# A hybrid block on one core: weight stream first in the engine orders, magnitude sums on ScalarE in place of maxima on VectorE, group operand sums on VectorE, other pacing

## The chip, the core and the metric

The kernel runs on one core of a Trainium2 chip. The core has five engines that each work through their own list of instructions in order: TensorE (PE in the profile, matrix products, with a second row PEld for its weight loads), VectorE (DVE), ScalarE (ACT), GpSimd (POOL) and SyncE (SP, which here only issues transfers). An instruction that has to wait for another engine, a buffer or a transfer holds up everything behind it in its list. The metric is the device time of one execution in microseconds (us). The kernel before took 3001.04, 3008.76 and 3016.93 us in three runs, so its median is 3008.76 us. The profiled execution took 2998.34 us.

## What is computed

One layer of a sequence model over 2048 latent and 256 context tokens of 1024 channels. The reference, cut to its core:

```python
h = modulate(x, norm1_g, shift1, scale1)                  # RMSNorm, scaled and shifted by c @ w_ada
u, g, p, gt = split(h @ w_in)                             # 1024, 1024, 512 and 2048 columns
uc = depthwise_conv(u)                                    # 4 taps
for d in (forward, backward):                             # gated linear recurrence
    r, i = sigmoid(uc @ w_r[d] + b_r), sigmoid(uc @ w_i[d] + b_i)   # 16 blocks of 64x64
    a = exp(-8 * r * softplus(-lam)); b = sqrt(1 - a*a) * (i * uc)
    h_lru += scan(a, b, start=final state of the context tokens)
pm = pool_mixer(p)                                        # windows 2, 4, 8, 16 in rows of 64
z = h_lru * gelu(g)
y = (sigmoid(gt[:1024]) * (z @ w_lru_out) + sigmoid(gt[1024:]) * (pm @ w_pool_out)) @ w_o
x = x + gate1 * y
x = x + gate2 * (square(relu(modulate(x, norm2_g, shift2, scale2) @ w1)) @ w2)
return rms_norm(x, final_g)
```

Inputs, outputs and weights are float32.

## The kernel before

**Numbers in two halves.** Each operand of a large product is scaled by a power of two and written as a float16 high part and a float16 rest. A product is three float16 matmuls (high by high, high by rest, rest by high; `mm3`, L78 to L85). The power of two comes from a bound on the magnitude: per partition a maximum (`absmax`, L104, on VectorE), a matmul with ones that adds the 128 partitions (L93, tile `sm`, a single bank of PSUM), and three small VectorE instructions on its result (L97, L99, L101). ScalarE then writes the high part (L108) and VectorE the rest (L109). For an input weight the maximum is `wm` (L124, L522), for the convolved channels `um` (L618), for a finished product of recurrence and gate `zmax` (L682).

**First part, the branches** (matmuls of L83, up to 1182 us of the trace). The modulated input stays on chip. An iteration over 8 groups of 128 channels (L740 to L755) does for group j: the gates of the recurrence (matmuls on `slot` by `g`, sigmoids L638), with the u columns of the next group between them; the coefficients and scans (L654 to L667, ScalarE, VectorE and GpSimd); the loads of the next input weights (`fetch`); the convolution of the next group, its `um` and its split (L610 to L622); one fill (sigmoid gate columns, evacuated from PSUM by ScalarE, L567, and stored); and the gate columns with GeLU (L678), times the recurrence (L680, L681) and out to memory. PSUM has 7 banks for these products. The pool branch follows.

**Second part, the merge** (1182 to about 1760 us). From here on products are in Winograd's form: 2x2 blocks with 7 products in place of 8 (`Job`, L938). Its operands need sums of blocks. Three groups of tokens (684, 684 and 680) go through the projections po, lo and wo. `from_dram` (L877) loads the four blocks of an operand into a tile F, forms three sums in four subtractions (`t_sums`, L853) on GpSimd, and splits the seven blocks (L863, L864).

**Third part, the MLP** (from about 1760 us): three groups through w1 and w2, matmuls of L957 again.

**The weight stream.** The weights of po, lo, wo, w1 and w2 are 44 units. Each is prepared once: loaded raw (tile `praw`, `load_raw`, L239), bounded by two sums of magnitudes on ScalarE (L264), scaled, summed into its seven blocks on GpSimd (four instructions a quarter of 128 columns, L290 to L293, tiles `praw` and `psum`), split into halves by ScalarE (L296, L297) and VectorE (L300, two a quarter, tile `pout`), and stored to memory (L303, `st_...`). A quarter here is 128 of a unit's columns: four to a unit, two for the po units. Products load prepared units with L931 into `wu`, by `ensure`, always some units ahead of their use. `prepare` (L251) is a generator: each `yield` names a number of TensorE columns, and `pace` (L314), called after each product with its columns, runs the generator on when they are used up. So the stream is written into the program between the products. `ensure` runs it further where a unit is needed at once. In the first part there is one `praw` buffer, later there are two (`prep_pool`).

**What sets the order.** SyncE's list is the program's order (L61). For the other engines a scheduler orders instructions by when it expects them to be ready and by a priority, which follows the program's order; `tc.high_priority` puts instructions ahead. The sum matmul of the weight stream stays at its place in the program on TensorE (L95).

## Time and profile before

| | us |
|---|---|
| three runs | 3001.04, 3008.76, 3016.93 |
| profiled execution | 2998.34 |
| its span, first to last instruction | 2996.6 |
| TensorE busy | 2600.5 (87%) |
| VectorE busy | 2079.3 (69%) |
| ScalarE busy | 1401.2 (47%) |
| GpSimd busy | 989.2 (33%) |
| mean granted TensorE clock | 0.940 of full speed |

The chain of waits that ended last is TensorE's own for the most part, so what matters is where TensorE stands still. TensorE's idle time differs much between the three parts, and the rows below are therefore taken part by part. In a row of a group, the time after the bar is the engine's idle time just before these instructions, and what ended it.

### The profile page before, as it was taken

What the parts mean: (1) busy time and instruction counts of PE and PEld (TensorE: products, weight loads), DVE (VectorE), ACT (ScalarE), POOL (GpSimd) and SP (SyncE); (2) the same over time, 40 slices, a digit from 0 to 9 for tenths busy, and PEclk for the clock granted to TensorE, in tenths of its full rate; (3) what the DMA queues carried; (4) which work ended last, traced back from release to release, by engine and by line L of the source; (5) the groups of instructions that cost most, each with busy time, mean ns of one, the idle gap of its engine ahead of it and who ended that gap; (6) DMA issues with size and microseconds to landing.
All of it is one profiled execution on the core that took longest, in us unless ns stands there. A gap on an engine that the chain in (4) does not pass through costs nothing. (4 is left out here: it accounts for less than half of the span.)

```text
span 2996.6 us, 39247 instructions
## 1 busy us (share of the span) xinstructions
PE 2600.5 (87%) x15212; PEld 1513.3 (50%) x15212; DVE 2079.3 (69%) x3151; ACT 1401.2 (47%) x1912; POOL 989.2 (33%) x1103
## 2 busy tenths in 40 slices
PE   6798798787788798977677699999899999999997
PEld 2243344343343344644444466666566665566664
DVE  6759779876976865575846868786774657665656
ACT  4645664465558334455535655563432333432322
POOL 4513443452525413766847543331010000100001
PEclk9899999898899899989888899999899999999998
DMA  7022233132112325877578597775454343454442
GB/s 301 1 94 97 95 137 124 60 139 95 77 68 104 107 95 190 306 273 277 210 279 290 205 335 287 267 273 185 150 213 153 143 170 137 154 223 148 150 162 84
DMA packets 152572, 513.75 MB, mean 171 GB/s; under 512 B 14144, under 2 KB 55872, under 8 KB 148160
## 3 DMA queue, kind: packets, MB, share of 16 engines
q1 hardware_dynamic: 114640, 386.96, 36.1%
q10 hardware_dynamic: 37744, 124.27, 10.6%
q8 instruction: 119, 1.95, 0.3%
q14 instruction: 69, 0.57, 0.1%
HBM read 386.92 MB, written 124.26 MB: 171 GB/s over the span
## 5 line engine op out<-in xcount | busy, mean ns | idle before, releaser
L957 PE MATMUL mm<-C,wu 128*128 128x342 f16 (+1 forms) x10584 | 1602.1, 313 | 159.7 <-DVE xm L1021 33.2
L957 PEld LDWEIGHTS <-wu 128*128 128x128 f16 x10584 | 1041.6, 99 | 707.9 <-issue 131.4
L83 PE MATMUL mm<-A,w 128*128 128x512 f16 x3408 | 791.0, 392 | 65.3 <-ACT slot L567 22.4
L83 PEld LDWEIGHTS <-w 128*128 128x128 f16 x3600 | 362.7, 102 | 491.6 <-issue 101.2
L1021 DVE SCALAR_TENSOR_TENSOR xm<-mm,cs,xm 128x342 f32<-128x342 f32 (+1 forms) x672 | 371.9, 570 | 212.8 <-PE mm L957 204.1
L206 POOL TENSOR_TENSOR psum<-praw 128x128 f32<-128x128 f32 x336 | 226.7, 680 | 504.6 <-DVE pout L300 297.2
L1144 POOL TENSOR_TENSOR xm<-xm,E 128x342 f32<-128x342 f32 (+1 forms) x84 | 80.6, 985 | 921.7 <-ACT E L1143 921.7
L1004 ACT ACTIVATE E<-mm,ivj 128x342 f32<-128x342 f32 (+1 forms) x216 | 112.8, 540 | 289.3 <-PE mm L957 270.7
L296 ACT ACTIVATE pout<-praw,su 128x512 f16<-128x512 f32 x168 | 120.1, 717 | 254.1 <-POOL praw L291 111.6
L300 DVE SCALAR_TENSOR_TENSOR pout<-praw,su,pout 128x512 f16<-128x512 f32 x168 | 145.6, 869 | 97.8 <-ACT pout L296 94.2
L291 POOL TENSOR_TENSOR praw<-praw 128x128 f32<-128x128 f32 x168 | 127.9, 769 | 124.0 <-issue 65.9
L863 ACT ACTIVATE C<-F,sc_s 128x1368 f16<-128x1368 f32 (+1 forms) x96 | 116.2, 1281 | 102.9 <-DVE sc_s L101 100.2
L1012 DVE SCALAR_TENSOR_TENSOR F<-mm,ivj,E 128x342 f32<-128x342 f32 (+1 forms) x144 | 81.2, 568 | 117.0 <-PE mm L957 106.0
L300 DVE SCALAR_TENSOR_TENSOR pout<-psum,su,pout 128x384 f16<-128x384 f32 x168 | 143.6, 856 | 5.3 <-ACT pout L297 3.9
L206 DVE TENSOR_TENSOR F<-F 128x342 f32<-128x342 f32 (+1 forms) x240 | 127.0, 534 | 24.8 <-ACT F L1203 20.1
L864 DVE SCALAR_TENSOR_TENSOR C<-F,sc_s,C 128x1368 f16<-128x1368 f32 (+1 forms) x96 | 140.6, 1471 | 0.0
L83 PE MATMUL mm<-slot,g 128*128 128x512 f16 (+1 forms) x528 | 118.5, 370 | 15.3 <-ACT slot L638 11.7
L264 ACT ACTIVATE pout<-praw 128x1024 f16<-128x1024 f32 (+1 forms) x88 | 89.4, 1016 | 77.3 <-DMA st_w<-pout 26.1
L297 ACT ACTIVATE pout<-psum,su 128x384 f16<-128x384 f32 x168 | 101.3, 606 | 28.2 <-POOL psum L206 28.0
L638 ACT ACTIVATE slot<-mm,vec,ivg 128x512 f32<-128x512 f32 (+1 forms) x160 | 106.9, 736 | 11.8 <-PE mm L83 8.9
L1007 ACT ACTIVATE F<-mm,ivj 128x342 f32<-128x342 f32 (+1 forms) x48 | 26.0, 542 | 173.4 <-PE mm L957 173.4
L206 POOL TENSOR_TENSOR psum<-praw,psum 128x128 f32<-128x128 f32 x168 | 97.7, 589 | 6.3
(188 smaller groups left out, 2762.5 us busy)
## 6 DMA issues: line engine op xcount, KB each, us to landing
wu<-st_w SPq DMA_DIRECT2D x192, 896.0 KB, 6.3
st_w<-pout ACTq DMA_DIRECT2D x128, 448.0 KB, 4.9
praw<-in_w_dram SPq DMA_DIRECT2D x96, 256.0 KB, 5.5
slot<-in_w_ada_dram SPq DMA_DIRECT2D x22, 1024.0 KB, 8.7
wu<-st_lo SPq DMA_DIRECT2D x24, 896.0 KB, 10.5
wu<-st_wo SPq DMA_DIRECT2D x24, 896.0 KB, 11.0
s<-slot ACTq DMA_DIRECT2D x11, 1024.0 KB, 3.9
xm<-s SPq DMA_DIRECT2D x32, 342.0 KB, 9.6
```

The lines of the kernel that those rows point to most:

```text
L83: TE.matmul(ps, l, r, start=(c == 0), stop=(c == n - 1))
L206: e.tensor_tensor(o, x, y, op=OP.subtract)
L291: G.tensor_tensor(r[:, 3, c], r[:, 3, c], r[:, 2, c], op=OP.add)
L296: S.activation(u[q][:, 0, 0:4, :], r[:, :, c], AF.Copy, scale=su)
L297: S.activation(u[q][:, 0, 4:7, :], f[q], AF.Copy, scale=su)
L300: V.scalar_tensor_tensor(u[q][:, 1, lo:hi, :], x, su, u[q][:, 0, lo:hi, :], op0=OP.mult, op1=OP.subtract)
L638: S.activation(dst[:, o:o + w], ps[:, :w], AF.Sigmoid, bias=vcol("br" if i == 0 else "bi", 8 * d + j), scale=self.ivg)
L863: S.activation(c[:, 0, lo:hi, :w], f[:, lo:hi, :], AF.Copy, scale=s)
L864: V.scalar_tensor_tensor(c[:, 1, lo:hi, :w], f[:, lo:hi, :], s, c[:, 0, lo:hi, :w], op0=OP.mult, op1=OP.subtract)
L957: TE.matmul(ps, l, r, start=(first and k == 0 and i == 0), stop=(k == self.m - 1 and i == 2), skip_group_check=(bank != "Y"))
L1004: S.activation(e[n], ps, AF.Copy, scale=iv)
L1021: V.scalar_tensor_tensor(o, ps, cs(r), o, op0=OP.mult, op1=OP.add)
```

## The change

Five edits. (1) Every step of the weight stream is now issued at high priority (`advance`), where before only its scale was. (2) The maxima over input weights (`prep`, `small_weights`), convolved channels (`conv`) and finished products (`gate`) become sums of magnitudes by ScalarE's Abs with an accumulated output; the elementwise output goes into a tile that is written later anyway, or is no longer needed. (3) `from_dram`'s block sums go from GpSimd to VectorE. (4) A speed factor multiplies the columns in `pace`: 1.25 in the first part, 0.6 in the second, 1.15 in the third. (5) Two yields differ: 5000 in place of 5500 a step, and 12000 in place of 5000 after a unit where there is one `praw` buffer. The maxima in `pool_sums`, `pool_mix` and a few small ones stay.

```diff
--- before.py
+++ after.py
@@ -116,12 +116,14 @@
     def prep(srcs, joint=False, w16=None):
 
         k = len(srcs)
-        raws, m = [], sm.tile([P, k], F32, name=f"wm{k}")
+        raws, ts, m = [], [], sm.tile([P, k], F32, name=f"wm{k}")
         for i, src in enumerate(srcs):
             n = src.shape[-1]
             raw = ring.tile([P, 1024], F32, name="raw")
             nc.sync.dma_start(raw[:, :n], src)
-            absmax(m[:, i:i + 1], raw[:, :n])
+            t = ring.tile([P, 2, 1024], F16, name="w16") if w16 is None else w16[i]
+            S.activation(t[:, 0, :n], raw[:, :n], AF.Abs, accum_out=m[:, i:i + 1])
+            ts.append(t)
             raws.append(raw[:, :n])
         if joint:
             mj = sm.tile([P, 1], F32, name="wmj")
@@ -131,7 +133,7 @@
         out = []
         for i, raw in enumerate(raws):
             n = raw.shape[-1]
-            t = ring.tile([P, 2, 1024], F16, name="w16") if w16 is None else w16[i]
+            t = ts[i]
             split(t[:, 0, :n], t[:, 1, :n], raw, s[:, 0:1] if joint else s[:, i:i + 1])
             out.append(t)
         return out, inv
@@ -235,6 +237,7 @@
             prep_order += [("w2", 2 * q - 2), ("w2", 2 * q - 1)]
     prep_pool = [prep1, 1, 1, 2]
     rest = [0.0]
+    speed = [1.25]
 
     def load_raw(kind, i):
         pp, nraw, _, _ = prep_pool
@@ -267,8 +270,7 @@
             mj = sm.tile([P, 1], F32, name="wmj")
             V.tensor_tensor(mj, m[:, 0:1], m[:, 1:2], op=OP.add)
             yield 3000
-            with tc.high_priority(offset=PRIO):
-                s, inv = scale_of_(mj, 1, 14, True)
+            s, inv = scale_of_(mj, 1, 14, True)
             su = sm.tile([P, 1], F32, name="su")
             V.tensor_copy(su, s)
             V.tensor_copy(inv_u[:, BASE[kind] + i:BASE[kind] + i + 1], inv)
@@ -301,21 +303,22 @@
                                                    op0=OP.mult, op1=OP.subtract)
                     else:
                         nc.scalar.dma_start(t[:, q], u[q])
-                yield 5500
+                yield 5000
             stash[(kind, i)] = t
             if nraw == 1:
-                yield 5000
+                yield 12000
 
     prep_steps = prepare()
 
     def advance():
-        rest[0] += next(prep_steps, 1e12)
+        with tc.high_priority(offset=PRIO):
+            rest[0] += next(prep_steps, 1e12)
 
     def pace(columns):
 
         if rest[0] is None:
             return
-        rest[0] -= columns
+        rest[0] -= columns * speed[0]
         while rest[0] <= 0:
             advance()
 
@@ -519,7 +522,7 @@
         nc.sync.dma_start(raw, src)
         w16 = hcp.tile([P, 2, 512], F16, name="g16", bufs=2)
         m = sm.tile([P, 1], F32, name="wm1")
-        absmax(m, raw)
+        S.activation(w16[:, 0], raw, AF.Abs, accum_out=m)
         s, inv = scale_of(m, 1)
         split(w16[:, 0], w16[:, 1], raw, s)
         return w16, inv
@@ -615,9 +618,9 @@
             for k in range(1, 4):
                 V.scalar_tensor_tensor(uc, up[:, k:k + L], vcol("cw", 8 * k + j), uc, op0=OP.mult, op1=OP.add)
             um = sm.tile([P, 1], F32, name="um")
-            absmax(um, uc)
+            self.u16 = slot([P, 2, L], F16)
+            S.activation(self.u16[:, 0], uc, AF.Abs, accum_out=um)
             su, invu = scale_of(um, 1)
-            self.u16 = slot([P, 2, L], F16)
             split(self.u16[:, 0], self.u16[:, 1], uc, su)
             self.ivg = mul_small(invg, invu, 1, "ivg")
 
@@ -679,7 +682,7 @@
             z = self.h[1]
             G.tensor_tensor(z[:, 0:T], self.h[0][:, 0:T], z[:, 0:T], op=OP.add)
             V.tensor_tensor(z[:, 0:T], z[:, 0:T], gel, op=OP.mult)
-            absmax(zmax[:, j:j + 1], z[:, 0:T])
+            S.activation(gel, z[:, 0:T], AF.Abs, accum_out=zmax[:, j:j + 1])
             nc.scalar.dma_start(z_d[j], z[:, 0:T])
 
 
@@ -880,7 +883,7 @@
         f = f_tile(w)
         for src, sl in ((srcs[k], slice(0, 4, 3)), (srcs[k + half], slice(1, 3))):
             nc.sync.dma_start(f[:, sl, :], src[:, t0:t0 + 2 * w].rearrange("p (c t) -> p c t", c=2))
-        t_sums(G, f[:, 0, :], f[:, 1, :], f[:, 2, :], f[:, 3, :], f)
+        t_sums(V, f[:, 0, :], f[:, 1, :], f[:, 2, :], f[:, 3, :], f)
         return split_f(f, s, w)
 
     aff2 = affine(mod2[:, 2, :], mod2[:, 1, :], vc("g2"), 2, UP)
@@ -1263,6 +1266,7 @@
         for _ in range(n):
             next(it, None)
 
+    speed[0] = 0.6
     stages = [Stage(g) for g in range(3)]
     stages[0].y, stages[0].z = y_0, z_0
     for i in range(4):
@@ -1291,6 +1295,7 @@
             sg.wo(i)
             if nx:
                 nx.load_z(i)
+    speed[0] = 1.15
     for g in range(3):
         for p in range(8):
             if g or p:
```

In the first part the change moves ScalarE's instructions in each iteration. Here is ScalarE's list for the third convolution of the first part, before: `w_...` are split input weights, `g_...` the weights of the recurrence's gates, the L108 row with `slot` is the split of the convolved channels, L567 evacuates the fill and L678 the gate.

```order
L108 ACTIVATE w_2297<-raw,sc_s_2295 128x1024
L303 DMA st_po_2223<-pout 128x1792
L264 ACTIVATE pout,wm_2548<-praw 128x1024 x2
L108 ACTIVATE w_2312<-raw,sc_s_2310 128x1024
L108 ACTIVATE g_2317<-raw,sc_s_2326 128x512
L108 ACTIVATE slot<-slot,sc_s_2343 128x2312
L567 ACT_TABLE_LOAD
L567 ACTIVATE slot<-mm,ivf 128x512 x4
L678 ACT_TABLE_LOAD
L678 ACTIVATE slot<-mm,ivp 128x512 x2
```

And the same place in the list now, where L125, L525 and L622 are the new sums, and L570 is the old L567:

```order
L125 ACTIVATE w_2309,wm_2306<-raw 128x1024
L622 ACTIVATE slot,um<-slot 128x2312
L570 ACT_TABLE_LOAD
L570 ACTIVATE slot<-mm,ivf 128x512 x4
L125 ACTIVATE w_2324,wm_2321<-raw 128x1024
L525 ACTIVATE g_2338,wm_2339<-raw 128x512
L108 ACTIVATE w_2309<-raw,sc_s_2317 128x1024
L125 ACTIVATE w_2532,wm_2529<-raw 128x1024
L573 DMA s_5_150<-slot 128x2048
L108 ACTIVATE w_2324<-raw,sc_s_2332 128x1024
L108 ACTIVATE g_2338<-raw,sc_s_2347 128x512
L108 ACTIVATE slot<-slot,sc_s_2365 128x2312
```

The four evacuations of the fill have moved from behind the split of the convolved channels to behind their sum; the split of the gate weights (`w_2297` before, `w_2309` now) has moved from ahead of all this to behind the evacuations.

TensorE's list at the same place now, from the last matmul of the fill to the first ones of the gate (before, the four `sm` matmuls stood one by one between matmuls of the fill and the gate):

```order
L83 LDWEIGHTS w_1821
L83 MATMUL mm<-A_364,w_1821 128x512
L93 MATMUL sm<-wm_2306,ones 128x1
L93 MATMUL sm<-wm_2321,ones 128x1
L93 MATMUL sm<-wm_2339,ones 128x1
L93 MATMUL sm<-um,ones 128x1
L83 LDWEIGHTS w_2309
L83 MATMUL mm<-A_189,w_2309 128x512
```

The four sums stand together, and the gate's matmuls behind them need the split of `w_2309`. Such a row of four stands at three of the eight convolutions (the third, the fourth and the last); before, only the sixth has one. At the second, fifth, sixth and seventh the gate's weights are now split ahead of the sum over the channels.

In the second part SyncE's list changes in the number of raw loads. Before, in the third group of tokens, from the last loads of po on (`praw` is a raw unit, `wu` a prepared one, `xm` gate values):

```order
L248 DMA praw<-in_w_dram 128x2x256 x4
L931 DMA wu<-st_po_1912 128x3584
L1045 DMA xm<-s_0_153 128x2x340
L1045 DMA xm<-s_4_157 128x2x340
L931 DMA wu<-st_po_2223 128x3584
L1045 DMA xm<-s_1_154 128x2x340
L1045 DMA xm<-s_5_158 128x2x340
L248 DMA praw<-in_w_dram 128x2x256 x4
L931 DMA wu<-st_wo_4479 128x3584 x2
L1045 DMA xm<-s_2_155 128x2x340
L1045 DMA xm<-s_6_159 128x2x340
L931 DMA wu<-st_wo_4873 128x3584 x2
```

The same place now:

```order
L934 DMA wu<-st_po_1815 128x3584
L1048 DMA xm<-s_0_153 128x2x340
L1048 DMA xm<-s_4_157 128x2x340
L934 DMA wu<-st_po_2087 128x3584
L1048 DMA xm<-s_1_154 128x2x340
L1048 DMA xm<-s_5_158 128x2x340
L934 DMA wu<-st_wo_3940 128x3584 x2
L1048 DMA xm<-s_2_155 128x2x340
L1048 DMA xm<-s_6_159 128x2x340
L251 DMA praw<-in_w_dram 128x1024
L249 DMA praw<-in_w_dram 128x512 x2
L934 DMA wu<-st_wo_4283 128x3584 x2
```

Of the two raw loads within these rows one is left, further back. Counted by the matmuls on `wmj` in TensorE's list, 16 units are scaled ahead of the first product of the second part before and 20 now; in the second part 16 before and 10 now; in the third 12 before and 14 now.

## Rows read from the trace of the kernel before

**Rows 1.** Busy time, granted clock and DMA by part: PE, PEld, DVE, ACT, POOL, clock.

```profile
130.00:1182.00 1052.00, 902.00 (x4204) 425.39 (x4201) 784.80 (x797) 572.79 (x682) 395.19 (x312) 0.93 0.27 101
1182.00:1760.00 578.00, 442.59 (x2749) 278.74 (x2749) 375.41 (x613) 287.30 (x479) 376.19 (x495) 0.89 0.74 271
1760.00:2997.00 1237.00, 1171.09 (x7973) 777.22 (x7970) 820.48 (x1606) 475.76 (x652) 145.46 (x237) 0.98 0.51 185
```

**Rows 2.** What TensorE waited for, 1182 to 1760: total us, times, longest.

```profile
PE mm L957 <- ACT E L1004: 32.3, 12, 8.3
PE mm L957 <- DMA wu<-st_lo: 17.5, 4, 6.7
PE sm L93 <- DVE wmj L268: 17.0, 8, 5.6
...
PE mm L957 <- DMA wu<-st_po: 12.5, 3, 10.2
```

**Rows 3.** What SyncE's queue waited for, 1182 to 1760.

```profile
SPq L248 <- DVE pout L300: 224.3, 13, 34.3
```

**Rows 4.** SyncE's issues in order of time: start, us, line, transfer.

```profile
1548.45 1.07 SPq L931 DMA_DIRECT2D wu<-st_lo  x2
1573.86 0.33 SPq L248 DMA_DIRECT2D praw<-in_w_dram  x1
...
1575.44 1.63 SPq L882 DMA_DIRECT2D F<-z  x2
1577.17 1.31 SPq L931 DMA_DIRECT2D wu<-st_lo  x2
```

**Rows 5.** What TensorE waited for, 130 to 1182.

```profile
PE sm L93 <- DVE um L105: 34.4, 5, 10.6
...
PE mm L83 <- ACT slot L567: 22.4, 6, 12.3
```

**Rows 6.** Busy time around the third and the sixth convolution, columns as Rows 1.

```profile
331.00:398.00 67.00, 51.20 (x232) 23.53 (x231) 59.82 (x54) 30.17 (x34) 28.31 (x15) 0.90 0.32 116
...
640.00:718.00 78.00, 48.20 (x230) 23.77 (x228) 66.41 (x60) 33.20 (x38) 37.00 (x27) 0.80 0.20 75
```

**Rows 7.** VectorE's groups, 1182 to 1760: busy us, mean ns, idle before.

```profile
L300 DVE SCALAR_TENSOR_TENSOR pout<-praw,su,pout 128x512 f16<-128x512 f32 x63 | 54.8, 877 | 22.9 <-ACT pout L296 22.0 <-DMA praw<-in_w_dram 0.8
L300 DVE SCALAR_TENSOR_TENSOR pout<-psum,su,pout 128x384 f16<-128x384 f32 x63 | 51.7, 824 | 0.5 <-ACT pout L297 0.5
...
L206 DVE TENSOR_TENSOR F<-F 128x342 f32<-128x342 f32 x24 | 15.7, 655 | 3.8 <-ACT F L1170 3.5
```

**Rows 8.** GpSimd's groups, 1182 to 1760.

```profile
L206 POOL TENSOR_TENSOR F<-F 128x342 f32<-128x342 f32 (+1 forms) x56 | 54.0, 965 | 26.6 <-DMA F<-z 21.6 <-DMA F<-y 3.6
...
L291 POOL TENSOR_TENSOR praw<-praw 128x128 f32<-128x128 f32 x64 | 33.0, 527 | 32.5 <-issue 17.8 <-ACT pout L264 14.1
```

**Rows 9.** VectorE's groups, 130 to 1182.

```profile
L300 DVE SCALAR_TENSOR_TENSOR pout<-psum,su,pout 128x384 f16<-128x384 f32 x56 | 60.2, 1075 | 4.8 <-ACT pout L297 3.4
L300 DVE SCALAR_TENSOR_TENSOR pout<-praw,su,pout 128x512 f16<-128x512 f32 x56 | 53.8, 962 | 51.5 <-ACT pout L296 48.8 <-DMA s<-slot 2.6
...
L105 DVE TENSOR_REDUCE wm<-raw 128x1 f32<-128x1024 f32 (+1 forms) x37 | 40.0, 1099 | 36.5 <-DMA raw<-in_w_gl_dram 21.8 <-DMA raw<-in_pool_w_dram 7.1 <-DMA raw<-in_w_gt_dram 3.9
...
L105 DVE TENSOR_REDUCE um<-slot 128x1 f32<-128x2312 f32 (+1 forms) x12 | 29.5, 2460 | 0.1
...
L105 DVE TENSOR_REDUCE zmax<-slot 128x1 f32<-128x2048 f32 x8 | 18.2, 2281 | 0.1
```

**Rows 10.** ScalarE's groups, 130 to 1182.

```profile
L108 ACT ACTIVATE w<-raw,sc_s 128x1024 f16<-128x1024 f32 x32 | 36.6, 1147 | 22.2 <-DVE sc_s L101 22.2
...
L108 ACT ACTIVATE slot<-slot,sc_s 128x2312 f16<-128x2312 f32 (+1 forms) x12 | 25.8, 2148 | 113.8 <-DVE sc_s L101 113.8
L567 ACT ACTIVATE slot<-mm,ivf 128x512 f32<-128x512 f32 x41 | 25.5, 686 | 17.6 <-PE mm L83 17.5
```

**Rows 11.** GpSimd's groups, 130 to 1182.

```profile
L291 POOL TENSOR_TENSOR praw<-praw 128x128 f32<-128x128 f32 x55 | 67.6, 1229 | 46.5 <-ACT pout L264 38.7 <-issue 4.7
```

## The prediction

> **What bounds the kernel now.** I read the busy times by part first. TensorE is idle for 1052 - 902 = 150 us in the first part, 578 - 443 = 135 us in the second and 1237 - 1171 = 66 us in the third [rows 1]. The second part is the worst: 23% idle in a fifth of the time, and the granted clock is lowest there (0.89 of full speed, so some of it at 1.2 GHz in place of 2.4). The third part is 95% busy and has little to give. So each edit is judged by TensorE's idle time in the first two parts.
>
> In the second part no engine is full: VectorE 65%, GpSimd 65%, ScalarE 50%, DMA 74% [rows 1]. I then asked what TensorE waited for. The rows name late weights (17.5 and 12.5 us on prepared units of lo and po), the weight stream's own sum matmul `wmj`, 17.0 us, and evacuations by ScalarE, 32.3 us [rows 2]. Late weights have a cause one step back. SyncE, whose list is in program order, stood at the raw loads of the weight stream for 224.3 us in 13 waits, 17 us each, until VectorE had finished with an earlier raw unit (L300) and its buffer was free [rows 3]. The issues in order of time show one such wait: after the load of 1548.45 nothing leaves until 1573.86, when the raw load goes; the next prepared weights of lo, which do not depend on it at all, leave at 1577.17 [rows 4]. A low-priority VectorE instruction holds the buffer, the raw load holds SyncE, and TensorE's weights stand behind it.
>
> In the first part TensorE waited for the channel maximum `um`, 34.4 us, and for banks that ScalarE had not evacuated from the fill, 22.4 us [rows 5]. A stretch from one gate section to the next shows why: from 331 to 398 us VectorE is busy 59.8 of 67 us and TensorE only 51.2, and from 640 to 718 it is 66.4 of 78 and 48.2 [rows 6]. VectorE is the bound in these stretches.
>
> **The change, part by part: second part.** Pacing sets how many units are prepared here. A unit cost 8000 + 3000 + 4000 + 7 x 5500 = 53,500 columns, or 156 matmuls of 342; now it costs 50,000 / 0.6 = 83,300, or 244. The part's products have some 2500 matmuls, so 16 units become 10, as the order counts. The 63 quarters of before [rows 7] become 40. That takes 23 x (0.877 + 0.824) = 39 us off VectorE. The block sums of `from_dram` come onto it: 56 instructions [rows 8], at 0.655 us as VectorE does the same shape elsewhere [rows 7], 37 us. So VectorE stays as it is, and GpSimd loses the 54 us that these took there [rows 8] and its share of the stream.
>
> What I expect of the waits: raw loads stand 88 matmuls further apart, and a raw unit is released sooner, since its last VectorE instructions now come first. Both shorten SyncE's 17 us. Late weights and `wmj` together are 17.5 + 12.5 + 17.0 = 47 us [rows 2]; I take off four fifths, 38 us (bounds 0 and 47, none being the case that the transfers themselves are slow). Of the 32.3 us of evacuations I take 8, a quarter: the stream is cut by 23/63, but at high priority what is left now stands ahead of evacuations (bounds: 32 off, 32 on). The clock: a matmul here took 442.59/2749 = 161 ns against 1171.09/7973 = 147 ns in the third part [rows 1], 39 us in all. With a third of the idle time (46 of 135 us) gone, a third of it comes back, 13 us. Against this, F's transfers were waited for by GpSimd, 26.6 us [rows 8], where little stood behind. Now VectorE waits for them, with evacuations queued behind it that TensorE needs. I charge 10 (bounds 0 and 27). Second part: -38 - 8 - 13 + 10 = -49 us.
>
> **First part.** Maxima that leave VectorE: 40.0 us of `wm`, 8 of 12 `um` at 2.460 = 19.7, and 18.2 of `zmax` [rows 9], 78 us. Sums that come to ScalarE are not in the trace in this place; nearest are its passes over like shapes, 1.147 us for 1024 elements, 2.148 for 2312 and 0.686 for 512 [rows 10], so 28 x 1.147 + 9 x 0.686 + 16 x 2.148, about 73 us. The weight stream's pace is a quarter faster (a unit's 30,000 + 15,000 + 13 x 5500 + 5000 = 121,500 columns become 30,000 + 15,000 + 13 x 5000 + 12,000 = 122,000, over 1.25 97,600). 20 units stand ahead of the second part instead of 16, which is 16 more quarters. On VectorE they cost 16 x (1.075 + 0.962) = 33 us [rows 9]. VectorE is relieved by 45 us and ScalarE goes, with its part of the stream (some 30 us), from 573 [rows 1] to some 680 of 1052 us, still below two thirds.
>
> Where it counts is in the bound stretches. By the order, from the second L657 of an iteration to the split of the next channels, 7 `um` and 8 `wm` go (26 us) and 17 instructions of the stream come (17 us): -9. Next, the fill is evacuated behind the channels' sum and no longer behind their split, so I take 17 of the 22.4 us [rows 5]. Against this, ScalarE's sum waits for VectorE's convolution, and at three convolutions the gate's weights are split only behind it: TensorE reaches the end of the fill and has nothing to do. Before, only the sixth convolution has its four sums in a row like that. That stretch left TensorE idle for 78 - 48 = 30 us, the third convolution's for 67 - 51 = 16 [rows 6]: such a stop costs up to 14 us. Three in place of one are 28 us at most (0 at least, where the matmuls held back are done while something else is waited for later); I take half, 14. First part: -9 - 17 + 14 = -12 us (bounds -57, all of rows 5 gone, and +28, with one exception under the rivals).
>
> **Third part.** 14 units in place of 12, 7 quarters, 12 us of VectorE at the prices of rows 7, beside a TensorE that is 95% busy. Cover is VectorE's idle third (820 of 1237 us busy [rows 1]); I charge 2 us (0 to 12). The first 130 us, with eight of the input maxima, I leave as they are.
>
> Sum: -49 - 12 + 2 = -59 on the profiled execution's 2998.3 us, 2939 us. The median of before lies 10 us above that execution, and single runs spread from 3001 to 3017. I add half of the 10 and forecast 2945 us, with its own range of 2885 to 2995.
>
> **A rival on the slow side: ScalarE's list stops TensorE at every convolution.** ScalarE already stood 113.8 us before its 12 splits of channels [rows 10]. The new sum stands ahead of the split, waits for the same convolution, and has evacuations and weight splits behind it at all eight. If TensorE stops at all of them at 14 us each, that is 112 - 14 = 98 us, and the 9 and 17 us above do not come: 2998 + 98 - 49 + 2 = 3049 us. It decides the sign from four further stops on, since 4 x 14 exceeds the other parts' gain. Against it: at the second, fifth, sixth and seventh convolution the gate's weights are split ahead, so TensorE has some 20 us of gate matmuls to do meanwhile. 15%.
>
> **A rival with a smaller gain: VectorE and GpSimd hold each other up.** The same GpSimd instruction (L291) takes 1229 ns in the first part [rows 11] and 527 in the second [rows 8], and VectorE's L300 1075 against 824 [rows 9, 7]. The first part gets 16 x 4 more GpSimd instructions, 34 us at 527 ns and 79 at 1229; if the mean of 56 falls on VectorE for the share of time that it is bound (seven stretches of some 65 us in 1052, 43%), 24 us come on top: first part +12, 2998 + 12 - 49 + 2 = 2963 us, 2970 with the offset. 20%. The Trainium skill's page "SBUF — State Buffer", under "Who interferes with whom", says that on trn2 a `tensor_reduce` never contends with GpSimd, while a VectorE instruction with two inputs in SBUF does, with the later one blocked throughout. By that rule the change removes VectorE time that disturbed nobody and adds time that does, which speaks for this rival; the rows show the two prices but not which VectorE instruction caused them.
>
> **A rival near no change: the second part keeps its waits.** DMA is 74% busy there at 271 GB/s [rows 1]; if loads are late by their number and not by SyncE's wait, and the evacuations stay as they are, only the 8 us come: 2998 - 12 - 8 + 2 = 2980, 2986 with the offset. Against it: the quiet of 25 us in rows 4. 12%.
>
> **How the numbers follow.** The forecast has 53%, the three rivals 15, 20 and 12. 0.5% (15 us) is about what a measurement of this kernel can tell from no change, so faster means below 2994, slower above 3024. The forecast's case lies below 2994 nearly always, the second rival in five of six, the third in half: 0.75. The slow rival with its nearer end gives most of slower: 0.13. Same: 0.12. For 8 in 10 I take 2875 to 3020: at the lower end all of the 47 us, all of rows 5 and half more of the 32 go (2945 - 9 - 45 - 16 = 2875), the upper one covers the two small rivals and the near end of the slow one.
>
> **What would show it.** Right: SyncE's waits at raw loads in the second part fall to a third or less of 224 us; TensorE's idle time there falls from 135 to some 90 us and the clock rises above 0.91; L300 counts some 40 quarters there. In the first part, waits of TensorE for L567 nearly vanish and those for `um`'s successor name ScalarE. Wrong: SyncE's waits are gone and TensorE is idle as before (then the evacuations were the cause); VectorE's sums on F wait long for transfers with L1021 behind them; TensorE's idle time in the first part exceeds 180 us (the slow rival); or GpSimd's L291 rises above 1229 ns there (the second).

## The result and the profile after

The changed kernel takes 2986.14 us (median of 6 runs, 2980.65 to 2988.14) against 3009.46 us (median of 6): a ratio of 0.9925, with a 95% interval of 0.9904 to 0.9947. One of the six runs of before was far slower than the others (3249.84 us), and the ratio leaves it out. The change makes the kernel faster, by 23 us where 64 were forecast. The profiled spans differ less, 2996.6 and 2984.3 us.

I take the parts apart by two events that every trace has: the first matmul of the merge (L957, now L960) and the last store of `rs` (L1134, now L1137).

| us | before | after | difference | forecast |
|---|---|---|---|---|
| first part, up to the first merge matmul | 1192.2 | 1242.8 | +50.6 | -12 |
| second part, up to the last store of `rs` | 596.1 | 510.4 | -85.7 | -49 |
| third part, to the end of the span | 1208.3 | 1231.1 | +22.8 | +2 |

So the second part gave more than forecast, and the first part, which was to give 12 us, lost 51. The second event doesn't cut TensorE's work at quite the same place: 2886 matmuls of the merge and MLP lie ahead of it before, 2839 after. Cut at the 2886th matmul in both, the second part differs by -78.8 us and the third by +16.0.

Busy time of after in the stretches of [rows 1]; columns PE, PEld, DVE, ACT, POOL, clock, DMA share, GB/s:

```profile
130.00:1182.00 1052.00, 869.68 (x4013) 412.67 (x4012) 722.12 (x753) 651.66 (x818) 466.78 (x344) 0.90 0.28 105
1182.00:1760.00 578.00, 495.01 (x3113) 311.76 (x3112) 411.23 (x686) 292.16 (x472) 311.13 (x392) 0.93 0.76 269
1760.00:2984.00 1224.00, 1151.95 (x7783) 761.67 (x7780) 810.25 (x1595) 464.06 (x635) 144.69 (x237) 0.97 0.51 184
```

From 130 to 1182 us TensorE did 191 matmuls fewer than before. VectorE did get its relief there, 785 to 722 us, and TensorE lost all the same. In the second row TensorE idles 83 us in place of 135 and the clock is 0.93 in place of 0.89. That row now holds 61 us of the first part; from the first merge matmul to the 2886th, TensorE idles 61 us in place of 125, at 0.94 in place of 0.90.

What TensorE waited for in the second part's stretch, against [rows 2]:

```profile
PE mm L960 <- DMA wu<-st_po: 22.3, 1, 22.3
PE mm L960 <- ACT E L1010: 15.3, 6, 5.8
PE mm L960 <- DVE C L1112: 14.0, 8, 3.1
...
PE mm L960 <- ACT E L1007: 6.7, 4, 4.0
```

The waits for `wmj` and lo are gone from the top; the 22.3 us for po is a single wait, at the part's first matmul (10.2 before). SyncE's queue in the same stretch, against [rows 3]:

```profile
SPq L934 <- PE mm L960: 217.3, 34, 19.1
```

No raw load waits for the stream's splits any more. SyncE now waits for a free `wu` buffer, that is, it has run ahead of TensorE, as the prediction wanted.

TensorE's waits in the first part, against [rows 5]:

```profile
PE sm L93 <- ACT w L125: 63.3, 6, 32.0
PE sm L93 <- DVE sc_e L97: 23.6, 17, 6.3
PE mm L83 <- ACT slot L641: 19.5, 10, 4.7
PE sm L93 <- DVE wmj L271: 18.4, 3, 16.4
PE sm L93 <- DVE um L105: 17.2, 2, 13.9
PE sm L93 <- ACT slot L622: 15.4, 3, 9.2
```

The waits for L567 (now L570) are gone. On top stands a new one: for the bound of an *input weight*, up to 32 us at a time. Around the longest, TensorE's list at the fourth convolution (start, us, then the idle time before in brackets):

```profile
452.78 20.88 PE L83 MATMUL mm<-A,w 128*128 128x512 f16 x96
505.64 0.58 PE L93 MATMUL sm<-wm,ones 128*128 128x1 f32 x2 [31.98 <-ACT w L125]
506.68 0.58 PE L93 MATMUL sm<-wm,ones 128*128 128x1 f32 x2 [0.46 <-ACT w L125]
507.61 0.56 PE L93 MATMUL sm<-wm,ones 128*128 128x1 f32 x2 [0.34 <-DVE sc_e L97]
508.42 0.59 PE L93 MATMUL sm<-um,ones 128*128 128x1 f32 x2 [0.25 <-DVE sc_e L97]
```

This is one of the three rows of four sums. ScalarE was not late with other work there; the weights were. SyncE's issues of the same trace:

```profile
411.13 3.21 SPq L537 DMA_DIRECT2D slot<-in_w_ada_dram  x4
497.06 0.34 SPq L251 DMA_DIRECT2D praw<-in_w_lo_dram  x1
497.45 0.91 SPq L249 DMA_DIRECT2D praw<-in_w_lo_dram  x2
498.40 0.43 SPq L123 DMA_DIRECT2D raw<-in_w_gl_dram  x1
498.87 0.43 SPq L123 DMA_DIRECT2D raw<-in_w_u_dram  x1
499.35 0.45 SPq L522 DMA_DIRECT2D raw<-in_w_g_dram  x1
```

From 414 to 497 us SyncE stood at a raw load of the stream, until VectorE's last split of the unit before (L302) freed the one `praw` buffer. The gate's weights (`in_w_gl`) are the next in its list and leave at 498, when TensorE has been idle for 25 us. It is the pattern of [rows 4], in the part where the prediction had not looked for it. The wait itself was there before, too (SyncE's queue of before, 130 to 1182 us; 973.5 us in 19 waits in after):

```profile
SPq L248 <- DVE pout L300: 833.1, 15, 135.1
```

The Trainium skill, page "DMA: Bandwidth & Descriptors", section "Anatomy of one DMA — SWDGE (gpsimd) path", has the rule behind this standing: a wait for a semaphore is done by the sequencer that issues the transfer, before it is dispatched. The issues above agree, on SyncE: nothing left for 83 us.

At the third and the last convolution it is the same (`in_w_gl` at 370 and 904 us, SyncE at a raw load for 69 and 65 us before). From one gate section to the next these three stretches take 75.9, 81.1 and 73.0 us in TensorE's list, four of the other five 57 to 61 (the remaining one holds the start of the pool branch). Before, one stretch of this kind had it: the sixth, 77.8 us, with `in_w_gl` at 666.5 behind a raw load.

What draws out the work on a raw unit can be read in the same stretch. GpSimd's sums of the stream and some VectorE instructions there (start, us):

```profile
467.40 2.62 DVE L619 SCALAR_TENSOR_TENSOR slot<-slot,vec 128x2312 f32<-128x2312 f32 x1
467.62 5.19 POOL L208 TENSOR_TENSOR psum<-praw 128x128 f32<-128x128 f32 x1 [11.03 <-DVE pout L302]
469.94 2.56 DVE L660 SCALAR_TENSOR_TENSOR slot<-slot 128x2312 f32<-128x2312 f32 x1
485.47 0.45 POOL L208 TENSOR_TENSOR psum<-praw 128x128 f32<-128x128 f32 x1
490.64 4.50 DVE L670 TENSOR_TENSOR_SCAN slot<-slot 128x2048 f32<-128x2048 f32 x1
490.94 4.45 POOL L293 TENSOR_TENSOR praw<-praw 128x128 f32<-128x128 f32 x1
496.41 4.94 POOL L683 TENSOR_TENSOR slot<-slot 128x2048 f32<-128x2048 f32 x1
497.13 4.63 DVE L302 SCALAR_TENSOR_TENSOR pout<-psum,su,pout 128x384 f16<-128x384 f32 x1
```

A sum by itself takes 0.45 us (485.47). The one at 467.62 starts just after a VectorE instruction with two inputs and ends only when that and the next such instruction are over; the one at 490.94 ends with a scan. Of the 268 sums from 130 to 1182 us, 92 took over 0.7 us, and 90 of these had begun while a VectorE instruction with two inputs of over 0.4 us was running; of the other 176 only 3 had. The last two rows show the other direction: a split, 0.60 us at 489.40, takes 4.63 beside a long GpSimd instruction of the recurrence.

### The profile page after: what moved, and what is told of

It is laid out like the page before. It is cut to its first block, busy times and chain, and to the rows that moved or that the text cites. A ratio compares the mean times of both kernels' runs of the same rounds, so it can differ in the third digit from the quotient of the medians.

```text
span 2984.3 us, 39437 instructions
## 1 busy us (share of the span) xinstructions
PE 2604.8 (87%) x15212; PEld 1519.4 (51%) x15212; DVE 2035.2 (68%) x3162; ACT 1477.5 (50%) x2035; POOL 995.2 (33%) x1031
## 4 chain that ended last, share of the span: by engine, by line
PE 40%; DMA 8%; DVE 7%; ACT 2%; issue 2%; POOL 1%; SPq 0%; ACTq 0%; DVEq 0%; POOLq 0%
PE mm L960 39%; DMA wu<-st_w 2%; DMA st_w<-pout 2%; DMA F<-z 1%; DVE F L208 1%; DVE pout L302 1%; DVE C L867 1%; DMA xm<-x 1%; PE mm L83 1%; DVE xm L1024 1%; DMA F<-y 1%; DVE C L1112 1%; DMA wu<-st_wo 1%; DVE C L208 1%; POOL psum L208 0%
## 5 line engine op out<-in xcount | busy, mean ns | idle before, releaser
L960 PE MATMUL mm<-C,wu 128*128 128x342 f16 (+1 forms) x10584 | 1599.9, 313 | 133.5 <-DMA wu<-st_w 25.2
L960 PEld LDWEIGHTS <-wu 128*128 128x128 f16 x10584 | 1041.7, 99 | 681.1 <-issue 102.1
L208 POOL TENSOR_TENSOR psum<-praw 128x128 f32<-128x128 f32 x336 | 252.0, 755 | 504.1 <-DVE pout L302 338.3
L302 DVE SCALAR_TENSOR_TENSOR pout<-praw,su,pout 128x512 f16<-128x512 f32 x168 | 164.3, 978 | 127.5 <-ACT pout L298 127.2
L208 DVE TENSOR_TENSOR F<-F 128x342 f32<-128x342 f32 (+1 forms) x312 | 171.4, 553 | 58.7 <-ACT F L1206 26.6
L293 POOL TENSOR_TENSOR praw<-praw 128x128 f32<-128x128 f32 x168 | 135.4, 812 | 131.5 <-issue 79.5
L302 DVE SCALAR_TENSOR_TENSOR pout<-psum,su,pout 128x384 f16<-128x384 f32 x168 | 138.4, 824 | 12.6 <-ACT pout L299 11.1
L267 ACT ACTIVATE pout<-praw 128x1024 f16<-128x1024 f32 (+1 forms) x88 | 89.3, 1015 | 98.2 <-DMA praw<-in_w_dram 41.7
L646 POOL TENSOR_TENSOR slot<-slot 128x2312 f32<-128x2312 f32 x16 | 100.6, 6285 | 50.1 <-ACT slot L641 41.7
L208 POOL TENSOR_TENSOR psum<-praw,psum 128x128 f32<-128x128 f32 x168 | 112.8, 676 | 7.8
```

The costliest lines, as they stand in the source:

```text
L208: e.tensor_tensor(o, x, y, op=OP.subtract)
L293: G.tensor_tensor(r[:, 3, c], r[:, 3, c], r[:, 2, c], op=OP.add)
L302: V.scalar_tensor_tensor(u[q][:, 1, lo:hi, :], x, su, u[q][:, 0, lo:hi, :], op0=OP.mult, op1=OP.subtract)
L646: G.tensor_tensor(I, I, uc, op=OP.mult)
L960: TE.matmul(ps, l, r, start=(first and k == 0 and i == 0), stop=(k == self.m - 1 and i == 2), skip_group_check=(bank != "Y"))
```

## Experiments

"Units" are how many of the 44 have their sum matmul in each part; the three times are the first merge matmul, the second and the third part, from the profiled execution. The ratio is to the kernel before on the same chip. That one execution lies up to 13 us off the median of its run (e5: 2936.46 us). The expectations cut the parts at matched places in TensorE's list, which ends the first part some 40 us earlier (about 1200 us for after) and counts one or two units in the third part that the table has in the second.

| run | units | first | second | third | median us | ratio, 95% interval |
|---|---|---|---|---|---|---|
| before | 16, 17, 11 | 1192.2 | 596.1 | 1208.3 | 3009.46 | |
| after | 20, 12, 12 | 1242.8 | 510.4 | 1231.1 | 2986.14 | 0.9925 (0.9904 to 0.9947) |
| e1 maxima on VectorE | 20, 12, 12 | 1277.8 | 508.5 | 1233.7 | 3020.94 | 1.0042 (1.0030 to 1.0055) |
| e2 no priority | 20, 12, 12 | 1238.7 | 507.3 | 1234.5 | 2988.56 | 0.9931 (0.9908 to 0.9953) |
| e3 old pacing | 16, 17, 11 | 1154.9 | 559.8 | 1232.1 | 2949.34 | 0.9801 (0.9778 to 0.9824) |
| e4 group sums on GpSimd | 20, 12, 12 | 1240.9 | 507.3 | 1232.2 | 2985.75 | 0.9924 (0.9896 to 0.9953) |
| e5 old pace in the first part | 16, 10, 18 | 1158.7 | 502.7 | 1273.3 | 2923.51 | 0.9717 (0.9691 to 0.9743) |
| e6 speed 1.00 | 16, 12, 16 | 1196.2 | 501.3 | 1261.5 | 2960.30 | 0.9826 (0.9809 to 0.9843) |
| e7 speed 0.85 | 14, 12, 18 | 1155.4 | 505.4 | 1272.5 | 2944.09 | 0.9770 (0.9747 to 0.9794) |
| e8 speed 0.70 | 12, 12, 20 | 1139.2 | 506.7 | 1332.3 | 2984.80 | 0.9914 (0.9894 to 0.9935) |
| e9 loads by ScalarE | 20, 12, 12 | 1222.9 | 500.5 | 1231.9 | 2957.97 | 0.9837 (0.9822 to 0.9852) |
| e10 e5 and loads by ScalarE | 16, 10, 18 | 1156.2 | 501.7 | 1271.4 | 2927.14 | 0.9731 (0.9715 to 0.9747) |
| e11 e9, second part 0.8 | 20, 15, 9 | 1223.3 | 532.8 | 1220.2 | 2977.04 | 0.9902 (0.9888 to 0.9917) |
| e12 e5, second part 0.8 | 16, 14, 14 | 1154.5 | 520.3 | 1219.9 | 2896.74 | 0.9630 (0.9616 to 0.9645) |
| e13 e9 without splits | 20, 11, 13 | 1208.7 | 512.0 | 1232.5 | 2962.26 | 0.9842 (0.9812 to 0.9873) |
| e14 e9 without sums | 20, 12, 12 | 1152.7 | 508.7 | 1234.1 | 2900.38 | 0.9637 (0.9609 to 0.9665) |
| e15 e12, third part 1.4 | 16, 14, 14 | 1157.0 | 515.8 | 1263.5 | 2936.77 | 0.9756 (0.9729 to 0.9783) |
| e16 speed 0.85, second 0.8 | 14, 15, 15 | 1156.6 | 533.2 | 1238.9 | 2931.39 | 0.9745 (0.9713 to 0.9777) |
| e17 e9, gap after sums | 20, 12, 12 | 1232.4 | 506.9 | 1231.3 | 2971.58 | 0.9882 (0.9866 to 0.9899) |
| e18 e12, gap after sums | 16, 14, 14 | 1176.4 | 521.2 | 1219.1 | 2918.57 | 0.9705 (0.9690 to 0.9719) |

### Each edit undone: e1 to e4

```diff
e1, four places (two in prep and small_weights, conv, gate)
-            S.activation(self.u16[:, 0], uc, AF.Abs, accum_out=um)
+            absmax(um, uc)
e2
-        with tc.high_priority(offset=PRIO):
-            rest[0] += next(prep_steps, 1e12)
+        rest[0] += next(prep_steps, 1e12)
e3
-    speed = [1.25]      (and 0.6, 1.15; yields 5000 and 12000)
+    speed = [1.0]       (and 1.0, 1.0; yields 5500 and 5000)
e4
-        t_sums(V, f[:, 0, :], f[:, 1, :], f[:, 2, :], f[:, 3, :], f)
+        t_sums(G, f[:, 0, :], f[:, 1, :], f[:, 2, :], f[:, 3, :], f)
```

> The changed kernel with edit 2 undone: all four maxima are VectorE's again, the rest stays. Theory A (ScalarE's sums hold its list, and TensorE stops at the end of the fill): TensorE's last matmul of the first part, 1193 us in the changed kernel's trace (part end about 1200 by matched work, 1162 before), comes 30 to 60 us earlier, and the whole is 20 to 50 us faster than the changed kernel. Theory B (the heavier weight stream is what slows the first part): the first part stays within 10 us of 1200, or gets longer, since VectorE has 78 us more.

> The changed kernel with edit 1 undone: the weight stream at the program's own priority. Theory A: the first part changes by less than 10 us, and the second gets longer again because SyncE's waits at raw loads come back (over 100 us of them): the whole 10 to 30 us slower than the changed kernel. Theory C (priority itself costs the first part, its instructions stand ahead of scans and convolution): the first part gets 20 us or more shorter.

> The changed kernel with edits 4 and 5 undone: all speeds 1, old yields. Theory B: the first part (16 units in place of 20) is 25 us or more shorter than 1200. Theory A: it is at most 15 us shorter, the second part is 30 us or more longer (16 units in place of 10), the third some 15 us shorter (12 units in place of 14): the whole within 15 us of the changed kernel.

> The changed kernel with edit 3 undone: the block sums of from_dram on GpSimd. If they cost what I charged, the second part gets 0 to 10 us shorter here, since VectorE no longer waits for F's transfers; if GpSimd was what held the evacuations back, it gets 10 us or more longer.

The sums on ScalarE gain 35 us, all in the first part (1277.8 to 1242.8), so theory A of e1 falls. Priority and the group sums change nothing that these runs can tell; in e2 SyncE's waits at raw loads didn't come back, though its theory A expected them. The pacing costs 37 us on the whole: undoing it takes 88 us off the first part and gives 49 back to the second. There SyncE's waits return in e3 (SyncE's queue, 1124 to 1656 us):

```profile
SPq L251 <- DVE pout L302: 192.4, 11, 28.0
```

### How much stream in the first part: e5 to e8

```diff
e5 (0.6 and 1.15 stay; the first yield is that of all three parts)
-    speed = [1.25]
+    speed = [1.0]
-                yield 5000
+                yield 5500
-                yield 12000
+                yield 5000
e6, e7, e8 (the new yields stay)
-    speed = [1.25]
+    speed = [1.0]       (0.85 in e7, 0.7 in e8)
```

> The changed kernel with old yields and speed 1 in the first part, 0.6 and 1.15 kept behind it: 16, 9 and 19 units in the three parts, and no convolution with the four sums in a row. Theory S (stops: TensorE stands at the end of the fill where the order has the four sums in a row) and theory U (each unit in the first part costs some 19 us there by its VectorE and GpSimd time) both expect the first part to end within 8 us of 1125 by matched work, as with old pacing throughout. The second part should take some 496 us as in the changed kernel and not the 532 of old pacing, so the whole is 15 to 35 us below 2949.

> The changed kernel at speed 1 in the first part, new yields: 16, 10 and 18 units, with one row of four sums, at the sixth convolution. Theory S: the first part is 12 to 25 us longer than in the run with old yields, and all of it lies in the stretch around the sixth convolution. Theory U: as many units, so within 5 us of it.

> The changed kernel at speed 0.85 in the first part: 14, 10 and 20 units, no row of four sums. Theory U: the first part ends some 38 us before 1125. Theory S: within 15 us of 1125. The third part has 6 units more than the changed kernel: if a unit is hidden there, it takes 1253 us or less, otherwise more.

> The changed kernel at speed 0.7 in the first part: 12, 10 and 22 units, no row of four sums. Theory U: the first part ends some 76 us before 1125. Theory S: within 20 us of 1125. The third part gets late weights where 22 units are too many for its first group: then it is 30 us or more longer than 1253, otherwise not.

e5 and e6 have 16 units each and differ by 37.5 us in the first part: the number alone doesn't price it, and theory U misses. Theory S misses, too: it put 12 to 25 us into the sixth stretch alone. In e6 the gate's weights of the sixth convolution leave at 683 us, behind a raw load that stood for 78 us, and that stretch takes 76.7 us; at the fourth they leave at 445, 10 us after the stretch has begun, and it takes 75.6. In e5, e7 and e8 none of the first seven stretches is over 69 us, and none has these loads more than 1 us after its start. Units do cost too, but unevenly: from 16 to 14 (e5, e7) the first part loses 3 us, from 14 to 12 another 16. What leaves the first part turns up in the third. SyncE's queue in the third part, e5 and then e8:

```profile
SPq L934 <- DMA st_w<-pout: 116.2, 14, 22.2
```

```profile
SPq L934 <- DMA st_w<-pout: 225.0, 25, 24.7
```

In the third part prepared units are now loaded as soon as they are stored, and SyncE stands for the store.

### The late loads by themselves: e9 and e10

```diff
+    q0 = [False]          (set to True ahead of the second iteration)
-            nc.sync.dma_start(raw[:, :n], src)
+            (nc.scalar if q0[0] else nc.sync).dma_start(raw[:, :n], src)
```

> The changed kernel in all but one thing: from the second iteration of the first part on, the loads of input weights (tile raw, L123 and L522) are issued by ScalarE and no longer by SyncE. In the changed kernel's trace, at the third, fourth and eighth convolution the gate weights' loads leave SyncE right behind a raw load of the weight stream that stood there 69, 83 and 65 us for its buffer, at 370, 498 and 904 us, and TensorE's stretches at these convolutions are the three long ones (75.9, 81.1, 73.0 us; 57 to 61 otherwise). Theory L (the late loads are what stops TensorE, and the pacing only decides where a raw load falls in SyncE's list): the 20 units stay, the three stretches fall to some 60 us, about 50 us go: 2935 us (2915 to 2955). Theory P (a heavier weight stream in the first part costs by its own work on VectorE, ScalarE and GpSimd): all that work is still there, so at most 10 us go: 2975 to 2990. Third possibility: ScalarE now stands at its own issues until a buffer is free, with evacuations behind: above 2990.

> The same edit on the version with the old pace in the first part (16, 9 and 19 units; 2923.5 us), where no gate weight leaves late. Theory L: nothing to gain, 2915 to 2930. If another queue for these loads is worth something for a reason other than the late gate weights, it gains here as much as it does with 20 units: below 2900.

With 20 units the three stretches fall to 61.5, 62.2 and 69.0 us, 37 us in all, and 19.9 of them are left at the end of the first part; with 16 units and no late load nothing goes. The whole, 2958 us, lies 3 us above theory L's range and far below theory P's. So the loads behind the stream's raw loads are shown as the cause of the stops, but they are less than a quarter of the 88 us that the pacing cost this part: 1222.9 against 1156.2 us are left for the denser stream with its four more units. From 130 us to the first merge matmul TensorE idles 185.5 us in e9 and 129.1 in e10, so 56 of these 67 us are waiting.

### Which engine pays for the units: e13 and e14

Both leave out part of the stream's arithmetic in the first part, as their expectations say.

```diff
e13
-   for x, lo, hi in ((r[:, :, c], 0, 4), (f[q], 4, 7)):
+   for x, lo, hi in ((r[:, :, c], 0, 4), (f[q], 4, 7)) if nraw > 1 else ():
e14
+   f[q] = r[:, 0:3, c]
+   if nraw == 1:
+       continue
```

> The version with loads by ScalarE (20 units in the first part, 2958 us), and in the first part VectorE's two splits a quarter (the second halves of prepared units) are left out; the first half is stored twice, by two transfers. So the outputs are not the reference's. It takes some 72 x 2 us = 140 us of work off VectorE and releases a raw unit after GpSimd and ScalarE. Theory V (VectorE is the bound in the stretches, and four more units cost by its work): the end of the first part falls from 1180 to 1130 or below, the whole to 2910 or less. Theory G (GpSimd's sums are the price, by holding up VectorE or the recurrence): falls by less than 20 us, above 2935.

> The same version, and in the first part GpSimd's four subtractions a quarter are left out (the splits read the raw blocks in place of sums), so the outputs are not the reference's. It takes 72 x 4 instructions, about 230 us, off GpSimd in the first part; VectorE and ScalarE do the same instructions as before. Theory V: VectorE's work is all there, less than 20 us go, above 2935. Theory G: the first part falls from 1180 to 1130 or below, the whole to 2910 or less; then the remaining splits of VectorE (L302 of the changed kernel) must also get shorter.

Taking VectorE's splits away leaves the whole where it was (first part -14.2); taking GpSimd's sums away gives 70.2 us in the first part. So the time doesn't follow VectorE's work: some 104 us less of it (723.3 to 619.4 us busy, 130 to 1182 us) gave 14 us. e14 leaves out the sums of all twenty units, so its 70 us is not the price of four; with them gone, the part ends where e10 ends it with the sums of 16. ScalarE's queue shows a likely way: its conversions of the sums (`pout` L300 and L301, before L296 and L297) stand in its list ahead of evacuations and channel sums. What it waited for in 130 to 1182 us, in e9:

```profile
ACT pout L300 <- POOL praw L295: 114.8, 28, 17.5
ACT pout L301 <- POOL psum L210: 28.1, 28, 4.4
ACT slot L624 <- DVE slot L621: 24.5, 6, 8.5
```

in e13:

```profile
ACT pout L300 <- POOL praw L295: 63.4, 33, 5.1
ACT pout L301 <- POOL psum L210: 60.4, 33, 7.8
ACT slot L625 <- DVE slot L622: 35.2, 5, 12.7
```

and in e14, where no wait for GpSimd is left at the top:

```profile
ACT pout L303 <- DVE su L277: 40.0, 11, 6.6
ACT slot L627 <- DVE slot L624: 32.5, 7, 8.6
ACT pout L303 <- DMA st_w<-pout: 27.3, 10, 7.0
```

143 us of standing in e9 and 124 in e13 go with the sums, not with the splits; some of it comes back as other waits (40.0 us for `su`, 23.9 in e9, and 27.3 for the store). It can't be the whole price of the denser stream: e10, 67 us shorter, still stands 119 us at these conversions. The other way would be that GpSimd slows VectorE's instructions. VectorE's convolution and scans in the same stretch, in e9 (busy us, mean ns):

```profile
L621 DVE SCALAR_TENSOR_TENSOR slot<-slot,vec 128x2312 f32<-128x2312 f32 x24 | 64.1, 2669 | 0.1
...
L668 DVE TENSOR_TENSOR_SCAN slot<-slot 128x2048 f32<-128x2048 f32 x8 | 36.2, 4523 | 0.1
```

and in e14:

```profile
L624 DVE SCALAR_TENSOR_TENSOR slot<-slot,vec 128x2312 f32<-128x2312 f32 x24 | 64.7, 2696 | 0.1
...
L671 DVE TENSOR_TENSOR_SCAN slot<-slot 128x2048 f32<-128x2048 f32 x8 | 35.8, 4476 | 0.0
```

They take as long without GpSimd's sums as with them. Of the splits, which theory G expected to get shorter, the one with 512 elements did not (875 and 904 ns); the one with 384 did (1035 and 746), but it reads the raw block there and no longer the sums. This fits the rows at 467 to 497 us: the stream's sums are short, so it is they that wait for VectorE's long instructions. What holds VectorE is for the most part GpSimd's long instructions of the recurrence, which e14 keeps: from 130 to 1182 us of after, VectorE's instructions with two inputs took some 100 us more than the shortest of their kind would, some 90 of it in instructions that began beside such a long one and under 10 beside a sum.

### Giving the sums time: e17 and e18

```diff
-                yield 5000
+                yield (10600 if step % 3 == 0 else 1500) if nraw == 1 else 5000
```

> The version with loads by ScalarE and 20 units in the first part (2958 us), and in the first part the yield after the step that issues GpSimd's sums is 10600 columns and the others 1500, in place of 5000 each: the same columns a unit (5 x 10600 + 8 x 1500 = 65000 = 13 x 5000), all work kept, but the conversions come later behind their sums. Theory W (ScalarE stands at the conversions, with sums over channels and evacuations behind): its waits for GpSimd's sums, 110 and 26 us before, halve, and the first part falls from 1180 to about 1150: 2915 to 2940. Theory C (GpSimd's sums cost by slowing other engines' instructions): the waits may fall but the time stays, 2950 to 2965.

> The same edit on the fastest version so far (old pace, 16 units in the first part, 0.8 in the second part, 2896.7 us): 11100 and 2000 in place of 5500 (5 x 11100 + 8 x 2000 = 71500). Theory W: its ScalarE waits about 100 us for sums in the first part; with half of them gone 10 to 25 us are won: 2872 to 2887. Theory C: 2890 to 2903.

e17 and e18 both missed their ranges. e17 didn't do what it was for: ScalarE's waits for GpSimd stay at 131 us (106.5 and 24.9; 143 before), and the time rises by 14. In e18 they fall from 120 to 96 us, but `in_w_gl` at the fourth convolution now leaves at 445, behind a raw load, and that stretch takes 75.7 us in place of 55.6: the late load again. So the standing at the conversions is argued from e13 and e14, not shown by itself.

### Where the units are best: e11, e12, e15, e16

```diff
-    speed[0] = 0.6
+    speed[0] = 0.8        (e11, e12, e15, e16)
-    speed[0] = 1.15
+    speed[0] = 1.4        (e15)
```

> Loads by ScalarE with 20 units in the first part, and the stream's speed in the second part 0.8 in place of 0.6, so some 3 units come from the third part to the second. From the runs so far a unit costs the second part about 9 us (531.7 against 478.8 us for 15 and 9 units) and the third 6 us up to 19 units and 18 above (1256.9, 1294.2, 1349.6 us for 13, 19 and 22). Theory: a unit moved at this level is worth nothing: within 12 us of the run with 0.6.

> Old pace in the first part as in the 2923.5 us version, loads by SyncE, and speed 0.8 in place of 0.6 in the second part: about 3 units move from the third part, which has 19, to the second. By the prices of 9 us a unit in the second part and 6 to 18 in the third: 2923 + 27 - 18 to -54, so 2896 to 2932, middle 2915. If SyncE's waits at raw loads in the second part return with it (183 us in the third part's first stretch now, hardly any in the second): 2940 and above.

> The 2896.7 us version (old pace in the first part, speed 0.8 in the second) with 1.4 in place of 1.15 in the third part. In its first group of tokens the third part waits for prepared units that are stored just before they are loaded (wu from st_w). Theory: the units come earlier against their use, and these waits fall: 2880 to 2895. If SyncE's waits for raw buffers (L251) grow as much as those for stores shrink, nothing changes: 2892 to 2902; if raw loads and evacuations suffer from the denser stream, above 2902.

> New yields with speed 0.85 in the first part (14 units, no gate weight late) and 0.8 in the second, 1.15 in the third. Against the 2896.7 us version two units fewer in the first part, which was 8 us shorter so (1120 against 1128), and two more in the third, which pays 6 to 18 us for each there: 2896.7 - 8 + 12 to 36, so 2900 to 2925. Below 2897 would mean that a unit in the first part costs more than one in the third.

e12 is the fastest of all, 0.963 of before: four units that the third part had to wait for cost the second 17.6 us and save the third 53 (27 us together by the medians, since e5's traced execution took 13 us more than its median). From e9 to e11 the same step costs 32 and saves 12, so e11 missed, by 7 us; the third part had only 12 units to begin with. e16 missed as well, at 2931 us: two units fewer in the first part gained nothing there (1156.6 against 1154.5), and the second and third part took 13 and 19 us more. e15 missed its theory; its last possibility came, a time above 2902 us: the same 14 units, sooner, cost 44 us in the third part. The rows are SyncE's wait and TensorE's, in e12:

```profile
SPq L251 <- DVE pout L302: 152.3, 12, 22.2
```

```profile
PE mm L960 <- DMA wu<-st_w: 23.4, 7, 9.1
```

and in e15:

```profile
SPq L251 <- DVE pout L302: 203.2, 12, 23.4
```

```profile
PE mm L960 <- DMA wu<-st_w: 39.9, 10, 6.3
```

A denser stream stands longer at its raw loads, with the prepared weights behind. That wait of TensorE explains 16.5 of the 44 us; its idle time rises by 23 us in all (68.6 to 91.7), and the same 7833 instructions keep it busy 20.5 us longer, at a granted clock of 0.96 in place of 0.97.

## Why the prediction was right in direction and too large

**First part, the step that failed.** The prediction took "VectorE is the bound in these stretches" from [rows 6] and so priced four more units by VectorE's instructions alone, 17 us. Its terms for this part against the runs: the relief (26 us of maxima and 17 of evacuations, 43 in all) measured 36.0, from before to the version with 16 units and the sums on ScalarE (e10), where the stop of before's sixth convolution is gone as well; e1, which undoes the sums alone, gives 35. The four more units, 17 us, measured +66.7 (e10 to e9). The stops, 14 us for two more, measured +19.9 for three (e9 to after). Together that is +50.6 in place of -12. The units are the term that failed: by e13 VectorE's splits of all twenty units are worth 14 us, and by e14 the part ends 70 us earlier without GpSimd's sums, which the sum left at nothing and only a rival priced, at 24. 12 us of the 66.7 are the longer wait for the first po unit (22.5 us in e9 against 10.2 in e10). By which way the sums cost the rest stays open.

That VectorE is busy doesn't say what its work is worth: 78 us of maxima taken off it gave 35 us, 104 us of splits gave 14.

**The stops** stand at the three convolutions where the order showed four sums in a row, as forecast. Their cause was put on ScalarE's list; it is SyncE's, and the wait of 833.1 us was there to be read in the first part of before.

**Second part.** The mechanism held: the waits at raw loads are gone, idle time fell to 83 us (90 forecast), the clock rose to 0.93 (above 0.91). L302 still counts 50 quarters in the stretch where 40 were expected. The gain was sized too small, -49 against -85.7 (-78.8 cut at the same matmul). e1, e2 and e4 show none of it to hang on one of the other edits, and e3 puts 49 on the pacing; the other 36 came with the edits 1 to 3 under the old pacing, and which it was is open. The 10 us charged for VectorE waiting on F were nothing: e4 gives them back without gain.

**Third part.** +22.8 in place of +2 (+16.0 cut at the same matmul). No edit undone alone brings it back (1231.9 to 1234.5 in e1 to e4 and e9), and e12, with more units, is 11 us shorter. Why is not settled.

**The rivals.** The slow one, stops at every convolution, did not come, though its sign did: TensorE idled 182 us in the first part, just over the 180 named, with stops at three convolutions. The one near no change gave 2986 us, the measured time, but by waits of the second part that in fact went: the agreement is chance. The rival of VectorE and GpSimd gave 2970 us and placed the cost with GpSimd's share of the stream, as e14 does. The two do hold each other up (the rows at 467 to 497 us), but the price was put on the wrong side: VectorE's convolution and scans kept their length in e14, and the stream's sums are what waits. The sign that it named did not come (L291, now L293, took 1135 ns, not over 1229), but it looks at one sum of four; all four together rose from 922 to 1015 ns in the mean, that is, from 104 to 151 us beyond 0.45 us each. The Trainium skill's page "SBUF — State Buffer", "Who interferes with whom", which this rival went by, says that a VectorE instruction with two inputs in SBUF contends with a GpSimd instruction that reads SBUF, and that the order of issue decides who is blocked. The rows above agree: the sum of 0.45 us takes 5.19 behind VectorE, the split of 0.60 us 4.63 behind GpSimd.

## What to carry to other kernels

A load that must wait for a buffer stops every load behind it in its queue; so look at what stands behind each such load in *every* part, and let the urgent loads go by another queue or ahead of it. A busy engine is not yet the bound, and a short instruction may take ten times as long beside a long one of another engine: leave out one engine's share of the suspect work and see whether the time moves. A background stream has a price per unit that differs by stage and rises with its density, so shift units between stages by measurement (here the pacing alone was worth 90 us, from 2986 to 2897).

## What the runs showed of the hardware

A sum of magnitudes on ScalarE is two instructions: at 487.01 us of the changed kernel L622 took 2.11 us for 2312 elements and a read of its accumulator another 0.19, together below VectorE's maximum over as many elements, 2.549 us in the trace of before (the 2.460 of [rows 9] is a mean with four shorter ones of 2048). GpSimd's sums of 128 elements took 1135 ns in the mean in the first part of the changed kernel (L293) and 629 in the second, 0.45 us each where no long VectorE instruction with two inputs ran. The stream's own splits are not what held them: the line took 890 ns in e9 with the splits and 934 in e13 without.
